# A two-layer hybrid decoder trunk on one core: gates computed with Tanh, one weight sum and two norm sums placed elsewhere

## The chip, the core and the metric

The kernel runs on one core of a Trainium2 chip. TensorE (PE) multiplies, VectorE (DVE) and ScalarE (ACT) work on elements, GpSimd (POOL) issues some transfers, and SyncE (SP) issues most of them through its own queue. The metric is the time of one execution on the device in microseconds; for the kernel before it is 2039.78 us, the median of three runs.

## The reference, cut to what matters

A sequence of 256 tokens of width 2048 goes through two layers. One input projection feeds three token mixers (A sparse attention, B a convolution module with a layer norm, C stick-breaking attention), a SiLU gate for each, and 3 x 2048 merge gates. All of it is float32.

```python
h = rms_norm(x, norm_w)
proj = h @ w_in                      # 2048 x 18064
(qa, ka, va, za, qi, ki, wi, ub, zb, qc, kc, vc, zc, gates) = split(proj)
y_a = (dsa_attention(...)            * silu(za)) @ w_a_out
y_b = (conformer_conv(ub, ...)       * silu(zb)) @ w_b_out
y_c = (stick_breaking_attention(...) * silu(zc)) @ w_c_out
g = sigmoid(gates).reshape(b, s, 3, 2048)
merged = g[:, :, 0] * y_a + g[:, :, 1] * y_b + g[:, :, 2] * y_c
x = x + merged @ w_out

# in conformer_conv, after the depthwise convolution (1024 channels):
y = layer_norm(y, ln_w, ln_b)        # mean, then mean of squares, over channels
```

## The kernel before

**Weight units.** Every product streams its weights. A unit is 256 x 512 weights, 128 partitions x 1024 floats, 512 KB. SP loads it into one of six `raw` buffers (`load_unit`, L270). ACT casts it into a high half (`high`, tile `wh`, L281), DVE subtracts that to get the low half (`low`, tile `wl`, L286), and PE makes three passes, high weight by both halves of the activations and low weight by their high half (`mult`, L297). There are three `wh` and three `wl` buffers, so a cast waits for PE to have read the `wh` three units back, and a load waits for DVE to have read the `raw` six units back. A regular unit has 12 matmuls of 512 columns.

**Work beside the stream.** Everything else (rotary, convolution, norms, attention) is written as generators. After each unit `background` lets one or two of them take a step; `yield n` says that the next step is due n units later. So the numbers behind `yield` place the work in the stream. The tile scheduler then sets the order of the instructions on each engine, by priority and by the ties that `issue_after` makes. A step that is placed on PE between two units stops the stream if its operands are not there yet.

**The norm of the convolution (`conv_norm`).** DVE folds eight channel groups into one tile, ACT writes its scaled high half (L1032, tile `ph`), DVE the low half, and `means` lets PE sum over partitions with a matrix of ones (L1038). That is done once for the mean and, after squaring (L1048), once for the mean of squares. Each time a `yield 3` stands between the fold and PE's sums. In the same stretch `attend` transposes the attention weights of mixer A by transfers (L994), and ACT copies the transposed halves back (L1002).

**Seven-product groups (`strassen`).** Three of the groups of merge-gate columns, `FAST = ((2, 0), (0, 0), (0, 1))`, each 1024 columns wide, are computed with seven products of blocks instead of eight. The activations are mixed once (`mix`); of the weights, sums of blocks are made on DVE (`summands`, L1195), then cast and split like a unit (`halves`). A product on such a block is 6 matmuls. The first half of a group runs four steps u, each with the blocks b11, b12 and b22 and with four products:

```python
product(o1, plain(0, 0), u, halves(b11));  s5 = summands(b11, b12);  yield 1
product(o5, mixed(0), u, halves(s5));      yield 2
b22 = block(KC, 512)                       # load
summands(s5, b22, dst=s6)                  # second sum, kept for the second half
product(o6, mixed(1), u, halves(s6));      s7 = summands(b12, b22);  yield 2
product(o7, mixed(3), u, halves(s7));      yield 2
```

After the four steps DVE and ACT combine the products (the first of the gates is activated at L1237); the second half has the other three products and activates the rest at L1254 and L1255. `combine` runs the regular units of the three branch outputs (`w_b`, `w_c`, `w_a`) and earns credit for each (`RATES`, 2.1 to 2.5 a unit); the group in turn spends it, `yield n` costing n. So a step with `yield 2` takes about the length of one regular unit.

**Gates.** The other merge-gate columns are regular units, and ACT applies the Sigmoid at L962 (`early_steps`). `combine` multiplies a branch's output by its gate and sums up (L1161, L1163, L1164). The SiLU gates of the branches are made in `gate_steps` (Silu at L439, product at L441). The stick-breaking heads (`stick`, two heads a call from h0) need Abs, Exp and Ln, and after each Abs the kernel asks for the table set with exp and ln (L770). ACT holds one set of function tables; where the next function is in another, an ACT_TABLE_LOAD stands in its order.

Of the kernel before, what the change touches and what calls it, by code (L numbers as in the profile page):

```python
# [53 lines left out]
def trunk(ctx: ExitStack, tc: tile.TileContext, x, xt, w_in, w_a, w_b, w_c, w_out,  # L54
          fnw, consts, out):
    nc = tc.nc
# [378 lines left out]
    def gate_steps(c0, o, b, w, hx, done, park=None, slots=(True, True), turn=TURN, need=(), ks=(0, 4)):  # L435
        def gated(k, z, v):
            for e in need:
                complete(e)
            nc.scalar.activation(v, z, AF.Silu)  # L439
            yield 1  # L440
            nc.vector.tensor_mul(z, v, o[:, k:k + 4, :])  # L441
            yield 1
            if park is None:
                b.extend(parts(4))
                h_, l_ = hi(b, k, 4), lo(b, k, 4)
            else:
                h_, l_ = v.bitcast(F32R), z.bitcast(F32R)
            nc.scalar.copy(h_, z)
            yield 1
            nc.vector.tensor_sub(l_, z, h_.bitcast(F32))  # L450
            if park is not None:
                for i, v_ in enumerate((h_, l_)):
                    nc.gpsimd.dma_start(park[:, k:k + 4, i], v_)

        for k in ks:
            a = yield from chunk_steps(w, [(c0 + k * P, 512)], hx, KD, whole=True)
            done.append(turn_in(a, None, partial(gated, k), slots[k // 4], turn))
# [66 lines left out]
    for layer in range(DEPTH):  # L524
# [234 lines left out]
        def stick(h0, qcT=qcT, kcT=kcT, vcr=vcr, diag=diag):  # L759
            ps = mm_tile()  # L760
            for q in range(2):
                nc.tensor.matmul(ps[:, q * S:(q + 1) * S], kcT[:, h0 + q, 0:P], qcT[:, h0 + q, :],
                                 start=True, stop=True)
            for q in range(2):
                nc.tensor.matmul(ps[:, 512 + q * P:512 + (q + 1) * P], kcT[:, h0 + q, P:S],
                                 qcT[:, h0 + q, P:S], start=True, stop=True)
            nk, lb = t4(), t4()
            ab = nc.scalar.activation(nk[:, :768], ps[:, :768], AF.Abs)
            with tc.issue_after(ab.ins):
                nc.scalar.preload_act_table_set("natural_log_exp_and_others")  # L770
            nc.scalar.activation(nk[:, :768], nk[:, :768], AF.Exp, scale=-1.0)
            yield 1
            nc.scalar.activation(nk[:, :768], nk[:, :768], AF.Ln, bias=1.0)
            yield 1
            nc.vector.scalar_tensor_tensor(lb[:, :768], ps[:, :768], 0.0, nk[:, :768],
                                           op0=ALU.min, op1=ALU.subtract)
            nc.vector.scalar_tensor_tensor(nk[:, :768], ps[:, :768], 0.0, nk[:, :768],
                                           op0=ALU.max, op1=ALU.add)
            yield 1
            for d in diag(nk):  # L780
                nc.vector.tensor_mul(d, d, smask2)
            pr_ = pair(768)
            nc.scalar.copy(pr_[0], nk[:, :768])
            yield 1
            nc.vector.tensor_sub(pr_[1], nk[:, :768], pr_[0].bitcast(F32))
            yield 3
            pc = mm_tile()
            for i, v in enumerate(pr_):
                nc.tensor.matmul(pc[:, :512], upper_r, v[:, :512], start=i == 0, stop=False)
            for i, v in enumerate(pr_):  # L790
                nc.tensor.matmul(pc[:, :512].rearrange("p (h t) -> p h t", h=2)[:, :, P:S], ones_r,
                                 v[:, 512:768].rearrange("p (h t) -> p h t", h=2), start=False, stop=i == 1)
            for i, v in enumerate(pr_):
                nc.tensor.matmul(pc[:, 512:768], upper_r, v[:, 512:768], start=i == 0, stop=i == 1)
            nc.vector.tensor_sub(lb[:, :768], lb[:, :768], pc[:, :768])
            yield 1
            nc.scalar.activation(lb[:, :768], lb[:, :768], AF.Exp)
            yield 1
            for d in diag(lb):
                nc.vector.tensor_mul(d, d, smask2)  # L800
            yield 2
            po = mm_tile()
            for q in range(2):
                vs_ = slice((h0 + q) * P, (h0 + q + 1) * P)
                nc.tensor.matmul(po[:, q * S:(q + 1) * S], vcr[:, 0, vs_], lb[:, q * S:(q + 1) * S],
                                 start=True, stop=False)
                nc.tensor.matmul(po[:, q * S + P:(q + 1) * S], vcr[:, 1, vs_],
                                 lb[:, 512 + q * P:512 + (q + 1) * P], start=False, stop=True)
            nc.scalar.copy(qcT[:, h0:h0 + 2, :], po[:, :512].rearrange("p (h t) -> p h t", h=2))
# [147 lines left out]
        def early_steps(b, j):  # L957
            a = yield from chunk_steps(w, [(O_G + b * D + j * 512, 512)], hx, KD)
            sg_ = t4().rearrange("p (t d) -> p t d", t=NT)
            with tc.high_priority():  # L960
                for t in range(NT):
                    nc.scalar.activation(sg_[:, t, :], a[t], AF.Sigmoid)  # L962
            nc.gpsimd.dma_start(gates[b][:, :, j * 512:(j + 1) * 512].rearrange("t p d -> p t d"), sg_)  # L963

        def attend(t, c, qaT=qaT, kaT=kaT, va=va, bias=bias):
# [56 lines left out]
        def conv_norm(cv=cv, pr=pr):  # L1022
            work = t4()
            ph_ = pair(512)[0]

            def fold(w_, first, second):
                w4 = w_.rearrange("p (c t) -> p c t", c=4)
                nc.vector.tensor_add(w4, first, second)
                nc.vector.tensor_add(w_[:, :512], w_[:, :512], w_[:, 512:])
                nc.vector.tensor_add(w_[:, :S], w_[:, :S], w_[:, S:2 * S])  # L1030
                h, l = ph_[:, :S], ph_[:, S:2 * S]
                nc.scalar.activation(h, w_[:, :S], AF.Copy, scale=1.0 / CW)  # L1032
                nc.vector.scalar_tensor_tensor(l, w_[:, :S], 1.0 / CW, h.bitcast(F32), op0=ALU.mult, op1=ALU.subtract)

            def means():
                ps = mm_tile()
                for i in range(2):
                    nc.tensor.matmul(ps[:, :S], ones_r, ph_[:, i * S:(i + 1) * S], start=i == 0, stop=i == 1)  # L1038
                return ps

            fold(work, cv[:, :4, :], cv[:, 4:, :])
            yield 3
            ps = means()
            sq = [t4().rearrange("p (c t) -> p c t", c=4) for _ in range(2)]
            for i in range(2):
                cs = cv[:, i * 4:i * 4 + 4, :]
                nc.vector.tensor_sub(cs, cs, heads(ps[:, :S], 4))
                nc.scalar.activation(sq[i], cs, AF.Square)  # L1048
                yield 1
            fold(work, *sq)  # L1050
            yield 3
            vs = means()
            r = rsqrt_mean(vs[:, :S], 1, t4())
            for i in range(2):
                cs = cv[:, i * 4:i * 4 + 4, :]
                yield 1
                nc.vector.tensor_mul(cs, cs, heads(r, 4))
                yield 1
                for c in range(4):
                    cc = i * 4 + c  # L1060
                    lw, lb = pr[:, P_LW + cc:P_LW + cc + 1], pr[:, P_LB + cc:P_LB + cc + 1]
                    nc.scalar.activation(cs[:, c, :], cs[:, c, :], AF.Silu, bias=lb, scale=lw)
# [70 lines left out]
        def combine():  # L1133
# [6 lines left out]
            for n, b in enumerate((1, 2, 0)):  # L1140
# [7 lines left out]
                for j in range(4):  # L1148
# [9 lines left out]
                    with tc.high_priority():  # L1158
                        dst = mg[j // 2][:, j % 2]
                        if n == 0:  # L1160
                            nc.vector.tensor_mul(dst, y, sg_)  # L1161
                        else:
                            nc.vector.tensor_mul(sg_, y, sg_)  # L1163
                            nc.vector.tensor_add(dst, dst, sg_)  # L1164
                    if n == 2 and j < 3:
                        mx[j], = parts(4)
# [37 lines left out]
        def strassen(b, jj):  # L1204
# [4 lines left out]
            for u in range(4):  # L1209
# [5 lines left out]
                s5 = summands(b11, b12)  # L1215
                yield 1
                product(o5, mixed(0), u, halves(s5))
                yield 2
                b22 = block(KC, 512)
                s6 = tp.tile([P, 1024], F32, tag=("ph", "pl")[u % 2], bufs=2, name=nm("s6")).rearrange(  # L1220
                    "p (k c) -> p k c", k=2)
                summands(s5, b22, dst=s6)
                kept.append(s6)
                product(o6, mixed(1), u, halves(s6))
                s7 = summands(b12, b22)
                yield 2
# [4 lines left out]
            with tc.high_priority():  # L1231
# [2 lines left out]
                nc.vector.tensor_sub(c12, o5, c21)  # L1234
                nc.vector.tensor_add(c21, o7, c21)  # L1235
                nc.vector.tensor_sub(c22, o5, c21)
                nc.scalar.activation(c22, c22, AF.Sigmoid)  # L1237
            yield 3
            pc, pd = mm_tile(), mm_tile()
            o2, o4, o3 = pc[:, :512], pc[:, 512:], pd[:, :512]  # L1240
# [9 lines left out]
            with tc.high_priority():  # L1250
                nc.vector.tensor_add(c11, o2, c11)
                nc.vector.tensor_add(c21, o4, c21)
                nc.vector.tensor_add(c12, o3, c12)
                nc.scalar.activation(res[0], res[0], AF.Sigmoid)  # L1254
                nc.scalar.activation(c12, c12, AF.Sigmoid)  # L1255
            if (b, jj) == fast[-1]:
                kept_res.extend(res)
                return
# [150 lines left out]
```

## Time and profile before

| | |
|---|---|
| median of three runs | 2039.78 us (2039.72 to 2040.48) |
| the profiled execution | 2038.03 us |
| its span, first to last instruction | 2036.3 us |
| mean granted TensorE clock | 0.997 |
| PE busy | 2009.3 us, 9518 matmuls |
| DVE busy | 1630.7 us |
| ACT busy | 1420.3 us, of it 31 table loads of 1.28 us |

In the listings a row names the line, the engine and the operation, then output<-inputs by the program's names, and the shape. A row of the timeline begins with the start and the length in us and may end with the idle time before it and what released it. A row of the windows has the window, its length, and for PE, PE's weight loads, DVE, ACT and POOL the busy time and the number of instructions, then the granted clock, the busy share of the DMA engines and the GB/s moved. A row of waits reads "engine, line waiting <- what ended the wait: us in total, times, longest". The first groups of the two layers run from about 605 and 1615 us, the norms' sums stand at about 526 and 1536 us.

### The profile page before, as it was taken

The page shows a single profiled execution, that of the slowest core. Times are in us where ns is not written, and L with a number is a line of the kernel's source. Part 1 is how long each engine was busy: PE and PEld are TensorE (multiplying, and loading weights), DVE is VectorE, ACT ScalarE, POOL GpSimd, SP SyncE. Part 2 cuts the span into 40 slices and gives each one's busy share as a digit, 9 for nine tenths or more (in the row PEclk, how much of TensorE's full clock was granted, in tenths as well). Part 3 has the DMA queues.
Part 4 walks back from the last instruction along what each step waited for, and adds up shares of the span by engine and source line. Part 5 has one row for each costly group of instructions (what it writes and reads, how often), then busy time and mean ns, then how long its engine had stood idle before and what let it go on. Part 6 is the DMA issues. An engine that isn't in the chain of part 4 may idle for free. (4 is left out here: it accounts for less than half of the span.)

```text
span 2036.3 us, 26826 instructions
## 1 busy us (share of the span) xinstructions
PE 2009.3 (99%) x9518; PEld 1684.6 (83%) x9518; DVE 1630.7 (80%) x1778; ACT 1420.3 (70%) x2000; POOL 102.9 (5%) x168
## 2 busy tenths in 40 slices
PE   9999999999999999999999999999999999999998
PEld 7888889988787788778888888899887877887787
DVE  8688767888898888896676887688887987889865
ACT  7699767559876656566657997675698756555653
POOL 0000000000000112200000000000000001212000
PEclk9999999999999999999999999999999999999999
DMA  8788657667898788889867775676777987889883
GB/s 282 214 226 217 178 157 227 206 198 200 213 262 243 247 272 290 281 251 262 257 202 219 212 214 168 170 224 197 206 203 211 271 254 238 269 289 296 245 273 126
DMA packets 349750, 466.98 MB, mean 229 GB/s; under 512 B 109360, under 2 KB 167472, under 8 KB 349488
## 3 DMA queue, kind: packets, MB, share of 16 engines
q1 hardware_dynamic: 329216, 425.01, 71.0%
q0 software_dynamic: 18944, 37.75, 6.2%
q10 hardware_dynamic: 1456, 2.51, 0.4%
q8 instruction: 74, 1.21, 0.3%
q14 instruction: 60, 0.49, 0.1%
HBM read 419.59 MB, written 23.07 MB: 217 GB/s over the span
## 5 line engine op out<-in xcount | busy, mean ns | idle before, releaser
L297 PE MATMUL acc<-wh,s 128*128 128x512 f32 (+2 forms) x4480 | 1099.2, 386 | 1.9 <-ACT wh L281 1.9
L286 DVE TENSOR_TENSOR wl<-raw,wh 128x1024 fp32r<-128x1024 f32 (+2 forms) x706 | 847.4, 1208 | 268.8 <-ACT wh L281 241.2
L297 PEld LDWEIGHTS acc<-wh,s 128*128 128x128 f32 x4480 | 828.1, 188 | 174.2 <-ACT wh L281 8.7
L281 ACT CAST wh<-raw 128x1024 fp32r<-128x1024 f32 (+2 forms) x705 | 729.6, 1039 | 320.7 <-PE acc L297 264.4
L297 PE MATMUL acc<-wl,s 128*128 128x512 f32 (+2 forms) x2240 | 590.7, 385 | 0.4 <-DVE wl L286 0.3
L297 PEld LDWEIGHTS acc<-wl,s 128*128 128x128 f32 x2240 | 415.0, 188 | 85.6 <-DVE wl L286 2.8
L476 ACT ACTIVATE t<-s,cst 128x255 f32<-128x255 f32 (+14 forms) x480 | 200.6, 488 | 0.0
L297 PE MATMUL mm<-wh,s 128*128 128x512 f32 x672 | 186.6, 397 | 10.2 <-ACT wh L281 8.7
L297 PEld LDWEIGHTS mm<-wh,s 128*128 128x128 f32 x672 | 124.7, 188 | 47.7 <-ACT wh L281 21.1
L479 DVE TENSOR_TENSOR s<-s,t 128x1020 f32<-128x1020 f32 (+14 forms) x120 | 138.6, 1155 | 1.9 <-ACT t L476 1.3
L297 PE MATMUL acc<-s,wh 128*128 128x384 f32 (+1 forms) x608 | 126.3, 348 | 0.0
L281 ACT CAST wh<-s 128x1024 fp32r<-128x1024 f32 x48 | 50.3, 1048 | 101.3 <-DVE s L1195 80.5
L297 PEld LDWEIGHTS acc<-s,wh 128*128 128x128 f32 x608 | 104.4, 189 | 3.2
L297 PE MATMUL mm<-wl,s 128*128 128x512 f32 x336 | 105.2, 394 | 0.3 <-DVE wl L286 0.3
L281 ACT CAST wh<-t 128x1024 fp32r<-128x1024 f32 x48 | 50.4, 1051 | 72.8 <-DVE t L1195 68.0
L286 DVE TENSOR_TENSOR wl<-s,wh 128x1024 fp32r<-128x1024 f32 x48 | 58.8, 1224 | 36.5 <-ACT wh L281 36.0
L297 PE MATMUL acc<-s,wl 128*128 128x192 f32 (+1 forms) x608 | 80.5, 273 | 0.0
L297 PEld LDWEIGHTS acc<-s,wl 128*128 128x128 f32 x608 | 79.5, 191 | 1.0
L297 PEld LDWEIGHTS mm<-wl,s 128*128 128x128 f32 x336 | 63.0, 189 | 15.0 <-DVE wl L286 1.5
L286 DVE TENSOR_TENSOR wl<-t,wh 128x1024 fp32r<-128x1024 f32 x48 | 58.8, 1224 | 20.0 <-ACT wh L281 19.0
L963 POOL DMA_DIRECT2D gates<-t x12 | 8.9, 742 | 1098.8 <-ACT t L962 1098.8
L248 POOL COPY sm<-sm 128x3 f32<-128x3 f32 x68 | 43.8, 652 | 400.7 <-ACT sm L247 400.7
(251 smaller groups left out, 1329.5 us busy)
## 6 DMA issues: line engine op xcount, KB each, us to landing
raw<-in_w_in_dram SPq DMA_DIRECT2D x578, 512.0 KB, 4.4
raw<-in_w_out_dram SPq DMA_DIRECT2D x64, 512.0 KB, 5.4
raw<-in_w_b_dram SPq DMA_DIRECT2D x32, 512.0 KB, 5.4
raw<-in_w_c_dram SPq DMA_DIRECT2D x32, 512.0 KB, 5.1
raw<-in_w_a_dram SPq DMA_DIRECT2D x32, 512.0 KB, 5.7
t<-gates POOLq DMA_DIRECT2D x20, 512.0 KB, 6.7
s<-parked POOLq DMA_DIRECT2D x32, 256.0 KB, 6.3
gates<-t POOLq DMA_DIRECT2D x12, 512.0 KB, 6.4
```

Of the source, the lines that this page charges most:

```text
L248: seen = nc.gpsimd.tensor_copy(copy[:, :3], mark)
L281: highs[0] = nc.scalar.copy(u[1], u[0])
L286: sub = nc.vector.tensor_sub(u[2], u[0], u[1].bitcast(F32))
L297: newest[0] = nc.tensor.matmul(o, lhsT, rhs, start=start, stop=stop, skip_group_check=True)
L476: nc.scalar.activation(o[:, i, :S - d], yT[:, c, :S - d], AF.Copy, scale=wq)
L479: sums.append(lambda: nc.vector.tensor_add(to, to, o[:, :, :S - d]))
L963: nc.gpsimd.dma_start(gates[b][:, :, j * 512:(j + 1) * 512].rearrange("t p d -> p t d"), sg_)
```

## The change

Four edits, with the same result up to rounding.

1. The merge gates are computed as tanh(x/2) in place of the sigmoid, which is (1 + tanh(x/2)) / 2. The 1 is added where the gate multiplies the branch's output, by a fused operation with the same number of instructions, and the factor 1/2 goes into the SiLU gate's product (L441), also a fused operation.
2. The request for the exp-and-ln tables in the stick-breaking heads stands only at h0 = 0.
3. In the first half of a seven-product group the load of b22 and the second sum stand ahead of the `yield 2` that was between the second and the third product.
4. The two `yield 3` ahead of the norm's sums become `yield 5`.

```diff
 gate_steps:
-            nc.vector.tensor_mul(z, v, o[:, k:k + 4, :])
+            nc.vector.scalar_tensor_tensor(z, v, 0.5, o[:, k:k + 4, :], op0=ALU.mult, op1=ALU.mult)
 stick:
-            with tc.issue_after(ab.ins):
-                nc.scalar.preload_act_table_set("natural_log_exp_and_others")
+            if h0 == 0:
+                with tc.issue_after(ab.ins):
+                    nc.scalar.preload_act_table_set("natural_log_exp_and_others")
 early_steps:
-                    nc.scalar.activation(sg_[:, t, :], a[t], AF.Sigmoid)
+                    nc.scalar.activation(sg_[:, t, :], a[t], AF.Tanh, scale=0.5)
 conv_norm, twice:
-            yield 3
+            yield 5
 combine:
-                            nc.vector.tensor_mul(dst, y, sg_)
+                            nc.vector.scalar_tensor_tensor(dst, sg_, 1.0, y, op0=ALU.add, op1=ALU.mult)
...
-                            nc.vector.tensor_mul(sg_, y, sg_)
+                            nc.vector.scalar_tensor_tensor(sg_, sg_, 1.0, y, op0=ALU.add, op1=ALU.mult)
 strassen:
                 product(o5, mixed(0), u, halves(s5))
-                yield 2
                 b22 = block(KC, 512)
...
                 summands(s5, b22, dst=s6)
                 kept.append(s6)
+                yield 2
                 product(o6, mixed(1), u, halves(s6))
...
-                nc.scalar.activation(c22, c22, AF.Sigmoid)
+                nc.scalar.activation(c22, c22, AF.Tanh, scale=0.5)
...
-                nc.scalar.activation(res[0], res[0], AF.Sigmoid)
-                nc.scalar.activation(c12, c12, AF.Sigmoid)
+                nc.scalar.activation(res[0], res[0], AF.Tanh, scale=0.5)
+                nc.scalar.activation(c12, c12, AF.Tanh, scale=0.5)
```

The number of matmuls is the same, and so is that of DVE's, POOL's and SP's instructions; on ACT 18 of the 31 table loads are gone (L770 has 2 in place of 8, L962 2 in place of 6, L980, L1062 and L1237 none in place of 4, 2 and 2), and on DVE 36 plain multiplies have become fused ones. From L771 on the changed kernel's lines are numbered one higher.

The first place is ACT at the end of the first half of the first group in layer 1. L1237 and L962 (now L1238 and L963) are gates, L439 is the Silu of a branch's gate, `wh_...<-s_976` (now `s_973`) is the cast of a second sum. Before:

```order
L281 CAST wh_6007<-raw_6005 128x1024
L1237 ACT_TABLE_LOAD
L1237 ACTIVATE t_1039_5937<-t_1039_5937 128x512
L281 CAST wh_6018<-raw_6017 128x1024
L188 COPY t_1003_5774<-t_1004_5775 128x1024
L281 CAST wh_6040<-raw_6038 128x1024
L439 ACT_TABLE_LOAD
L439 ACTIVATE t_1004_5775<-t_1003_5774 128x1024
L962 ACT_TABLE_LOAD
L962 ACTIVATE t_1064_6061<-acc_5778 128x512
L281 CAST wh_6051<-s_976_5647 128x1024
```

and with the change:

```order
L281 CAST wh_6015<-raw_6014 128x1024
L188 COPY t_1003_5771<-t_1004_5772 128x1024
L1238 ACTIVATE t_1039_5934<-t_1039_5934 128x512
L281 CAST wh_6037<-raw_6035 128x1024
L439 ACTIVATE t_1004_5772<-t_1003_5771 128x1024
L281 CAST wh_6048<-s_973_5625 128x1024
L281 CAST wh_6074<-raw_6073 128x1024
L247 COPY sm_6067<-wh_6048 128x3
L963 ACTIVATE t_1064_6058<-acc_5775 128x512
```

The three loads are gone, and the gate of L963 stands behind the cast of the sum and one more.

The second place is DVE in the second step of the first group. `wl_...` are lows, `t_969` is the first sum (s5), `s_976` (now `s_973`) the second (s6), `t_979` the third (s7); the low from `raw_5626` (now `raw_5627`) belongs to a regular unit. Before:

```order
L286 TENSOR_TENSOR wl_5605<-raw_5600,wh_5604 128x1024
L1195 TENSOR_TENSOR t_969_5614<-raw_5600,raw_5602 128x1024
L286 TENSOR_TENSOR wl_5617<-t_969_5614,wh_5616 128x1024
L286 TENSOR_TENSOR wl_5628<-raw_5626,wh_5627 128x1024
L1195 TENSOR_TENSOR s_976_5647<-t_969_5614,raw_5645 128x1024
L286 TENSOR_TENSOR wl_5650<-s_976_5647,wh_5649 128x1024
L1195 TENSOR_TENSOR t_979_5659<-raw_5602,raw_5645 128x1024
```

and with the change:

```order
L286 TENSOR_TENSOR wl_5602<-raw_5597,wh_5601 128x1024
L1196 TENSOR_TENSOR t_969_5611<-raw_5597,raw_5599 128x1024
L286 TENSOR_TENSOR wl_5614<-t_969_5611,wh_5613 128x1024
L1196 TENSOR_TENSOR s_973_5625<-t_969_5611,raw_5623 128x1024
L286 TENSOR_TENSOR wl_5629<-raw_5627,wh_5628 128x1024
L286 TENSOR_TENSOR wl_5647<-s_973_5625,wh_5646 128x1024
L1196 TENSOR_TENSOR t_979_5656<-raw_5599,raw_5623 128x1024
```

The second sum stands ahead of the regular unit's low; on SP the load of its block (`raw_5645`, now `raw_5623`) stands ahead of the regular unit's load in the same way.

The third place is ACT and PE at the norm of layer 1. On ACT before (`ph_4711`, now `ph_4708`, is the scaled copy; `wh_4816`, `wh_4840` and `wh_4881` are casts of the fifth, sixth and eighth unit of a block of the regular stream, now `wh_4806`, `wh_4835` for the fifth and sixth):

```order
L281 CAST wh_4840<-raw_4839 128x1024
L991 COPY t_800_4720<-t_782_4625 128x512 x3
L281 CAST wh_4863<-raw_4862 128x1024
L991 COPY t_800_4720<-t_782_4625 128x512
L1002 COPY t_770_4563<-t_771_4564 128x512 x2
L281 CAST wh_4881<-raw_4880 128x1024
L1032 ACTIVATE ph_4711<-t_797_4710 128x256
```

and with the change:

```order
L1003 COPY t_770_4560<-t_771_4561 128x512
L281 CAST wh_4806<-raw_4805 128x1024
L992 COPY t_800_4717<-t_782_4622 128x512 x4
L281 CAST wh_4835<-raw_4834 128x1024
L1003 COPY t_770_4560<-t_771_4561 128x512
L1033 ACTIVATE ph_4708<-t_797_4707 128x256
```

The scaled copy stands behind the cast of the sixth unit instead of the eighth; one of the copies of transposed words is directly ahead of it. PE's sums stood after three and after eight matmuls of the sixth unit (`wh_4840`):

```order
L297 MATMUL acc_4725<-wl_4817,s_10_101 128x512 x4
L297 MATMUL acc_4725<-wh_4840,s_10_101 128x512 x3
L1038 MATMUL mm_4784<-ph_4711,ones_r 128x256
L297 MATMUL acc_4725<-wh_4840,s_10_101 128x512 x5
L1038 MATMUL mm_4784<-ph_4711,ones_r 128x256
```

and stand now ahead of it:

```order
L297 MATMUL acc_4722<-wl_4807,s_10_101 128x512 x4
L1039 MATMUL mm_4827<-ph_4708,ones_r 128x256 x2
L297 MATMUL acc_4722<-wh_4835,s_10_101 128x512 x8
```

So, counted in units of this block, the sums stand on PE three to eight matmuls earlier than before, with the larger number behind `yield`.

More of the change, by code (lines that the diff above doesn't have):

```diff
@@ L1050, in conv_norm @@
             fold(work, *sq)
-            yield 3
+            yield 5
             vs = means()
```

## The prediction

> **What bounds the kernel.** I read the mean granted clock and the busy shares first, then the busy time by windows of 100 us, then the waits of the engine that bounds, and at last the timeline around its longest waits.
>
> ```profile
> core 0: 2036.3 us, clock 0.997
> PE 2009.3 (99%) x9518; PEld 1684.6 (83%) x9518; DVE 1630.7 (80%) x1778; ACT 1420.3 (70%) x2000; POOL 102.9 (5%) x168
> ```
>
> TensorE (PE) is busy in 99% of the span, and PE's matmuls are counted with modelled ends, so a busy share near 100% still hides lost time. The number of matmuls in a window is the sharper measure (columns: PE busy and count, weight loads, VectorE (DVE), ScalarE (ACT), POOL, granted clock, DMA share, GB/s):
>
> ```profile
> 100.00:200.00 100.00, 100.00 (x443) 82.81 (x442) 82.47 (x75) 96.60 (x178) 0.00 (x0) 1.00 0.83 221
> 600.00:700.00 100.00, 95.71 (x400) 74.30 (x399) 84.72 (x78) 65.46 (x69) 4.32 (x7) 0.98 0.81 240
> 700.00:800.00 100.00, 99.76 (x438) 81.57 (x437) 85.46 (x77) 56.02 (x71) 20.47 (x33) 1.00 0.83 267
> 800.00:900.00 100.00, 98.52 (x427) 79.20 (x426) 89.83 (x81) 56.42 (x73) 19.84 (x34) 1.00 0.92 293
> 1600.00:1700.00 100.00, 95.42 (x399) 74.13 (x398) 85.35 (x82) 65.98 (x70) 5.50 (x8) 0.98 0.83 235
> 1700.00:1800.00 100.00, 99.76 (x438) 81.62 (x437) 87.78 (x79) 55.57 (x69) 18.64 (x30) 1.00 0.86 280
> 1800.00:1900.00 100.00, 98.73 (x429) 79.31 (x428) 89.25 (x81) 57.32 (x76) 21.96 (x37) 1.00 0.90 288
> ```
>
> The undisturbed pace is 443 matmuls per 100 us, 0.226 us each. The windows with the first seven-product group (600 to 700 and 1600 to 1700) lack 43 and 44 matmuls, 87 x 0.226 = 19.7 us. The four windows with the second and third groups lack 5, 16, 5 and 14, that is 40 x 0.226 = 9.1 us (both counts from above, since a few records may be missing). That is all there is to win in the groups. What PE waits for by name (us in total, times, longest):
>
> ```profile
> PE mm L297 <- ACT wh L281: 8.7, 13, 2.3
> PE mm L1038 <- ACT ph L1032: 4.4, 2, 2.8
> PE acc L297 <- ACT wh L281: 1.9, 7, 0.3
> SPq L270 <- DVE wl L286: 1117.7, 553, 7.4
> ACT wh L281 <- DMA raw<-in_w_in_dram: 8.9, 6, 1.7
> ```
>
> PE waits for ScalarE's casts and twice for the norm's folded sum. The transfer queue waits 1117.7 us for free buffers, and the casts wait for transfers only 8.9 us: transfers run ahead.
>
> **Part one: gates by Tanh, 18 table loads fewer.** ACT has slack on the whole (70%), so a load counts only where PE waits for the cast behind it. There is one such place in each layer, at the end of the first half of the first group:
>
> ```profile
> 676.65 1.28 ACT L439 ACT_TABLE_LOAD   x1
> 677.94 1.06 ACT L439 ACTIVATE t<-t 128x1024 f32<-128x1024 f32 x1
> 678.04 1.07 PE L297 MATMUL mm<-wh,s 128*128 128x512 f32 x4
> 679.02 1.28 ACT L962 ACT_TABLE_LOAD   x1
> 680.32 0.60 ACT L962 ACTIVATE t<-acc 128x512 f32<-128x512 f32 x1
> 680.81 1.04 ACT L281 CAST wh<-s 128x1024 fp32r<-128x1024 f32 x1
> 681.90 1.53 PE L297 MATMUL mm<-wh,s 128*128 128x512 f32 x4 [2.34 <-ACT wh L281]
> 1692.54 1.78 PE L297 MATMUL mm<-wh,s 128*128 128x512 f32 x4 [2.34 <-ACT wh L281]
> 680.00:690.00 10.00, 8.10 (x28) 6.47 (x29) 6.82 (x7) 7.25 (x10) 1.83 (x3) 0.83 0.62 160
> 1530.00:1540.00 10.00, 7.25 (x33) 5.65 (x32) 7.92 (x11) 7.42 (x11) 0.00 (x0) 1.00 0.88 221
> 1690.00:1700.00 10.00, 7.66 (x27) 6.02 (x27) 6.90 (x7) 7.89 (x10) 1.77 (x3) 0.83 0.58 143
> ```
>
> Two loads (2 x 1.28 = 2.56 us) and the gate's first ACTIVATE (0.60) stand between the Silu and the cast that PE waits for, 2.34 us in each layer. In the changed order both loads are gone and the gate's ACTIVATE stands behind that cast. So the cast starts 3.1 us earlier; 2.34 us are needed. Right behind, the granted clock is 0.83 over 10 us, which is half clock for 3.4 us, a loss of 1.7 us. Without the idle the clock has no reason to drop: 2.34 + 1.7 = 4.1 us a layer, **8.2 us**. Bounds: 4.7 (idle alone) to 8.2.
>
> Here the Trainium skill, page "ScalarE: Activation LUTs", section "What ACT_TABLE_LOAD costs", speaks of about 1380 ns of drain beside the 1283 ns of the load. The rows above show no drain (677.94 follows 676.65 + 1.28 at once), so the measurement decides. By the page's 2.66 us a switch, an estimate, 18 loads would give ACT 47.9 us, against 18 x 1.28 = 23.1 by the rows.
>
> The other 14 loads I cost at nothing: the loads of the stick-breaking heads and of the early gates stand where PE lacks no matmul (443 per 100 us), under PE's 2.72 us a unit. If that cover failed, a load would be worth 1.28 us: at most 14 x 1.28 = 17.9 us, which I don't believe, since PE's list of waits has no such sum. A Tanh of 128x512 is priced like the Sigmoid it replaces, and the fused multiply like the plain one:
>
> ```profile
> L962 ACT ACTIVATE t<-acc 128x512 f32<-128x512 f32 x24 | 13.9, 594 | 4.3 <-PE acc L297 4.2
> L974 DVE SCALAR_TENSOR_TENSOR t<-mm,bias 128x1024 f32<-128x1024 f32 x4 | 4.9, 1222 | 4.1 <-DMA gates<-t 4.1
> L1163 DVE TENSOR_TENSOR t<-acc,t 128x1024 f32<-128x1024 f32 x16 | 19.5, 1220 | 0.5 <-PE acc L297 0.5
> ```
>
> 36 of them by 2 ns are 0.07 us: nothing.
>
> **Part two: the second sum a step sooner.** In each of the four steps of a group's first half DVE makes the second sum just before ACT casts it:
>
> ```profile
> 624.15 1.22 DVE L1195 TENSOR_TENSOR s<-t,raw 128x1024 f32<-128x1024 f32 x1
> 625.48 1.05 ACT L281 CAST wh<-s 128x1024 fp32r<-128x1024 f32 x1 [1.74 <-PE acc L297]
> 626.58 1.20 PE L297 MATMUL mm<-wh,s 128*128 128x512 f32 x4 [0.23 <-ACT wh L281]
> 637.56 1.20 PE L297 MATMUL mm<-wh,s 128*128 128x512 f32 x4 [0.79 <-ACT wh L281]
> ```
>
> Sum, cast and product are a chain with no room: the cast ends at 626.53, and PE starts 0.05 us later, after 0.23 us of idle. Now the sum stands ahead of the regular unit's low between (1.22 us), so the chain begins that much sooner. Nothing is added, DVE does the same 7 operations per step; the change moves work. What it pays: the 19.7 us of the first groups less the 8.2 above leave 11.5; part of it belongs to the first and third sums, which do not move (637.56 waits for a first sum). I take about two thirds, **7.5 us**, since the freed ACT time and the earlier sum both shorten these chains; bounds 0 and 11.5. Of the 9.1 us of the later groups I take **1.5** (bounds 0 and 5), because there PE's waits by name are tenths.
>
> Its cost: b22's raw load (SP's queue) moves ahead of a regular unit's load in 24 steps (4 steps, 3 groups, 2 layers). I put **1.5 us** as new stalls here (bounds 0 and 27, priced under the rivals); what covers it is the lead of the transfers above.
>
> **Part three: the norm's sums two units later.** PE's two matmuls for the mean stand in the middle of a unit, and their operand comes late:
>
> ```profile
> 519.17 2.32 SPq L994 DMA_TRANSPOSE t<-t  x1
> 524.79 0.76 ACT L1002 COPY t<-t 128x512 uint16<-128x512 uint16 x1 [1.31 <-DMA t<-t]
> 525.42 1.03 ACT L281 CAST wh<-raw 128x1024 fp32r<-128x1024 f32 x1
> 526.36 0.41 ACT L1032 ACTIVATE ph<-t 128x256 fp32r<-128x256 f32 x1
> 526.83 0.39 PE L1038 MATMUL mm<-ph,ones_r 128*128 128x256 f32 x1 [1.61 <-ACT ph L1032]
> 1537.20 0.39 PE L1038 MATMUL mm<-ph,ones_r 128*128 128x256 f32 x1 [2.75 <-ACT ph L1032]
> ```
>
> ACT's scaled copy stood behind a copy that waits for a transpose (1.31 us) and behind the cast of a unit two places ahead. Now it follows the cast of the sixth unit, with one such copy between, whose transposes SP issues earlier, and the sums stand behind the fifth unit on PE. I take the whole wait, **4.4 us**; bounds 4.4 and -1.4 (the first of the two, now 3 matmuls nearer the front, waits 3 x 0.226 = 0.7 us longer in each layer).
>
> **Sum.** 8.2 + 7.5 + 1.5 + 4.4 - 1.5 = 20.1 us. The profiled execution took 2038.03 us, 1.7 us of it outside the span, and lies 1.75 us under the median 2039.78. So the profile after should read 2017.9, and the median **2019.7**; with the first groups' sums between 3.5 and 11 us in place of 7.5 the likeliest case runs from 2016 to 2024.
>
> **Rivals.**
>
> Only the loads and the norm pay (15%). DVE is the cover here, 85 to 90% busy in all group windows, and a reordered sum only pushes the next low back by 1.22 us: what the second product gains the regular unit's low loses. Then 8.2 + 4.4 = 12.6 us stay, 2027.2. For it: DVE's count is unchanged, 84.72 of 100 us in the worst window. Against: every named wait of a product there is for ACT's cast, not for DVE's low.
>
> The norm's wait stays (15%): a transposed copy like the one that ACT waited 1.31 us for still stands directly ahead of the scaled copy. Then PE, which comes to its sums earlier, pays 1.4 more instead of 4.4 less, and the sum is 20.1 - 4.4 - 1.4 = 14.3, 2025.5. Against: the scaled copy stands two casts earlier, and the transposes leave SP earlier.
>
> The clock drops all the same (4%): the 3.4 us at half clock follow a 2.34 us idle, yet no drop followed 2.75 us at 1534 to 1537, where the granted clock is 1.00. So idle length alone does not decide, and shorter stalls could still bring it: 20.1 - 3.4 = 16.7, 2023.1. The Trainium skill, page "TensorE: Matmul & The Clock Gate", Part 1, has a free-running window of about 3.4 us, after whose idleness the rate halves; the trace has the 3.4 us, but a 2.34 us idle sufficed.
>
> Slower, through the transfer queue (9%). A unit's load lands 4.4 us after issue, and 512 KB at the mean rate take 524,288 B / 229 GB/s = 2.3 us:
>
> ```profile
> DMA packets 349750, 466.98 MB, mean 229 GB/s; under 512 B 109360, under 2 KB 167472, under 8 KB 349488
> raw<-in_w_in_dram SPq DMA_DIRECT2D x578, 512.0 KB, 4.4
> ```
>
> In 24 steps b22's load now goes ahead of a regular unit's, with six raw buffers for both, so that unit's weights come up to 2.3 us later. If half of it, 1.15 us, comes out uncovered, 24 x 1.15 = 27.5 us are lost: 2019.7 + 27.5 = 2047.2. It turns the whole change slower from 20.1 / 24 = 0.84 us a step. For it: DMA is 81 to 92% busy in these windows. Against: the casts' 8.9 us of waits for transfers in the whole span.
>
> **Chances.** Likeliest case 57%, the three milder rivals 15, 15 and 4%, the slower one 9%. A measurement of this kernel tells 0.2% (4.1 us, so below 2035.7 or above 2043.9) from no change. Faster by more: 57 + 15 + 15 + 4 = 91%. Of the slower rival two thirds lie above 2043.9: 6%, and 3% within. The range that should hold the time 8 times in 10 reaches down to the sums' full 11.5 us with 2 us more in the later groups (20.1 + 6 = 26.1, 2013.7) and up to the first rival with the half clock kept as well (2027.2 + 3.4 = 2030.6): 2013.5 to 2031.
>
> **What would show it.** Right: no wait of over 1 us of a product for ACT's cast near 676 to 684, granted clock 1.00 in that window, no wait of L1038's successor for the scaled copy, 13 table loads on ACT, and some 435 matmuls in the windows of the first groups (4.1 + 3.75 us are 35 more than 400). The sums' term is wrong if the count there rises by only 18, the 4.1 us of the loads and the clock, while the second products no longer wait; the slower rival shows as casts that wait for raw transfers, by tens of us. The forecast falls if the first groups lack as many matmuls as now, or if the stall at the norm only moves to the next unit.

## The result, and the profile after

The changed kernel takes 2011.84 us (median, 2011.18 to 2013.56), the kernel before 2039.75 us in the same comparison: a ratio of 0.9866, with an interval of 0.9849 to 0.9883, so 27.9 us faster. Faster was forecast, by 20.1 us; the time lies 1.7 us below the range. The profiled execution after took 2011.18 us, 26.85 us less than the one before.

First the granted clock, the busy shares, and the windows of 100 us around the norms (500, 1500) and the groups (columns as before: window, length, PE busy and count, weight loads, DVE, ACT, POOL, clock, DMA share, GB/s):

```profile
core 0: 2009.4 us, clock 0.999
PE 1997.0 (99%) x9518; PEld 1685.5 (84%) x9518; DVE 1626.4 (81%) x1778; ACT 1399.2 (70%) x1982; POOL 110.0 (5%) x168
500.00:600.00 100.00, 100.00 (x444) 82.75 (x443) 87.23 (x96) 82.89 (x113) 3.79 (x6) 1.00 0.87 236
600.00:700.00 100.00, 99.63 (x434) 80.57 (x433) 90.69 (x84) 67.70 (x75) 8.41 (x15) 1.00 0.87 262
700.00:800.00 100.00, 100.00 (x443) 82.76 (x442) 87.22 (x79) 57.90 (x74) 21.97 (x35) 1.00 0.87 279
800.00:900.00 100.00, 99.23 (x432) 80.16 (x431) 91.78 (x84) 58.78 (x70) 17.43 (x24) 1.00 0.87 276
1600.00:1700.00 100.00, 99.58 (x434) 80.55 (x433) 90.99 (x84) 66.81 (x75) 9.17 (x15) 1.00 0.87 263
1700.00:1800.00 100.00, 100.00 (x442) 82.78 (x442) 88.54 (x80) 58.44 (x74) 21.11 (x33) 1.00 0.88 282
1800.00:1900.00 100.00, 99.63 (x434) 80.73 (x433) 92.35 (x84) 59.98 (x71) 17.43 (x24) 1.00 0.88 274
```

The windows of the first groups went from 400 and 399 matmuls to 434 each, as expected (435). The windows from 700 and 1700 are at the undisturbed pace, which was not expected to that extent. ACT is less busy by 21.1 us, close to the 23.1 of the loads. What PE's products still wait for by name:

```profile
PE mm L297 <- ACT wh L281: 0.9, 3, 0.5
PE acc L297 <- ACT wh L281: 0.9, 3, 0.5
```

The timeline at the end of the first half of the first group, and at the norm of layer 1:

```profile
668.84 1.05 ACT L439 ACTIVATE t<-t 128x1024 f32<-128x1024 f32 x1
670.11 1.22 DVE L1196 TENSOR_TENSOR s<-s,raw 128x1024 f32<-128x1024 f32 x1
671.34 1.07 PE L297 MATMUL acc<-wl,s 128*128 128x512 f32 x4
671.41 1.05 ACT L281 CAST wh<-s 128x1024 fp32r<-128x1024 f32 x1 [1.52 <-DVE s L1196]
672.24 1.07 PE L297 MATMUL mm<-wh,s 128*128 128x512 f32 x4
673.41 0.59 ACT L963 ACTIVATE t<-acc 128x512 f32<-128x512 f32 x1
...
520.14 0.81 ACT L1003 COPY t<-t 128x512 uint16<-128x512 uint16 x1
520.77 0.45 ACT L1033 ACTIVATE ph<-t 128x256 fp32r<-128x256 f32 x1
524.02 0.40 PE L1039 MATMUL mm<-ph,ones_r 128*128 128x256 f32 x2
```

The cast at 671.41 no longer stands behind loads and the gate. It waits 1.52 us for DVE's sum, and PE goes on without a gap. At the norm the scaled copy is done at 521.2 and PE reads it at 524.0, 2.8 us later. The list of waits has no row for L1039.

For the comparison of many kernels I use one figure by stage: the time by which matmuls start later after the one before than at the undisturbed pace of their form, summed over the stage and both layers. It is worked out from the start times in each profile, so from one execution of each kernel, which lies up to 2.5 us off the kernel's median. "Rest" is nearly the same everywhere and belongs to other stages. Counted instead by when the matmul of the same number starts in the profiles before and after, the norms gain 1.9 and 3.1 us in the two layers, the first groups 7.8 and 8.0, the later groups 2.7 and 2.9: a stage's figure is good to about 0.8 us.

| lost time in us | norm | first groups, first half | its end | second groups, first half | up to the third groups' end | rest | sum |
|---|---|---|---|---|---|---|---|
| before | 7.8 | 9.8 | 10.1 | 2.2 | 7.9 | 26.9 | 64.7 |
| the change | 2.0 | 4.1 | 0.0 | 0.0 | 5.1 | 27.0 | 38.1 |
| gates only (e1) | 5.5 | 9.9 | 2.2 | 2.8 | 7.7 | 26.7 | 54.8 |
| second sum only (e2) | 6.8 | 4.1 | 1.7 | 0.1 | 5.8 | 27.2 | 45.6 |
| yields only (e3) | 9.4 | 9.5 | 10.4 | 2.2 | 7.7 | 27.1 | 66.3 |
| gates and sum (e4) | 4.4 | 4.1 | 0.0 | 0.1 | 5.1 | 27.1 | 40.7 |
| gates and yields (e5) | 2.8 | 9.9 | 1.8 | 2.9 | 7.8 | 26.6 | 51.7 |
| sum and yields (e6) | 6.6 | 4.1 | 1.7 | 0.0 | 5.2 | 27.3 | 44.9 |
| b22's load only (e7) | 10.0 | 8.9 | 11.2 | 4.3 | 8.0 | 27.0 | 69.4 |
| the change and first sum (e8) | 1.8 | 0.1 | 0.0 | 0.0 | 3.1 | 27.2 | 32.1 |
| first sum only (e10) | 8.3 | 5.1 | 9.4 | 0.0 | 3.1 | 26.6 | 52.4 |
| e8 and fourth sum (e11) | 2.0 | 1.1 | 0.0 | 1.0 | 3.9 | 27.0 | 34.9 |

### The profile page after: what moved, and what is told of

Its sections match the earlier page's. It is cut to its first block, busy times and chain, and to the rows that moved or that the text cites. A ratio compares the mean times of both kernels' runs of the same rounds, so it can differ in the third digit from the quotient of the medians.

```text
span 2009.4 us, 26811 instructions
## 1 busy us (share of the span) xinstructions
PE 1997.0 (99%) x9518; PEld 1685.5 (84%) x9518; DVE 1626.4 (81%) x1778; ACT 1399.2 (70%) x1982; POOL 110.0 (5%) x168
## 4 chain that ended last, share of the span: by engine, by line
PE 93%; DVE 3%; ACT 1%; issue 1%; DMA 1%; ACTq 0%; DVEq 0%; SPq 0%
PE acc L297 80%; PE mm L297 10%; DVE wl L286 1%; ACT wh L281 1%; DMA raw<-in_w_c_dram 1%; DVE t L1196 1%; PE mm L941 1%; PE mm L971 1%; PE mm L1011 0%; DVE s L1196 0%; PE mm L806 0%; PE mm L762 0%; DMA raw<-in_w_in_dram 0%; PE mm L915 0%; PE mm L790 0%
## 5 line engine op out<-in xcount | busy, mean ns | idle before, releaser
L297 PE MATMUL mm<-wh,s 128*128 128x512 f32 x672 | 182.2, 391 | 1.1 <-ACT wh L281 0.9
L248 POOL COPY sm<-sm 128x3 f32<-128x3 f32 x68 | 51.4, 765 | 382.0 <-ACT sm L247 382.0
```

The costliest lines, as they stand in the source:

```text
L248: seen = nc.gpsimd.tensor_copy(copy[:, :3], mark)
L297: newest[0] = nc.tensor.matmul(o, lhsT, rhs, start=start, stop=stop, skip_group_check=True)
```

## The experiments

The change has three parts that can be taken apart: the gates with their table loads (edits 1 and 2), the second sum with its block's load (edit 3), the yields (edit 4). The theory of the prediction is that each pays at its own place. The rival is that they stand in for one another or need one another. Six kernels make all combinations, with before and the change. Each is compared with the kernel before on its own chip; differences below are to that median.

**Gates only.** Edits 1 and 2 on the kernel before.

```diff
-  nc.scalar.activation(sg_[:, t, :], a[t], AF.Sigmoid)
+  nc.scalar.activation(sg_[:, t, :], a[t], AF.Tanh, scale=0.5)
...
+  if h0 == 0:
```

> The kernel before with the gates by Tanh and the 18 table loads gone, the second sum and the yields of the norm as before. If the parts pay each at its own place (the prediction): the 2.34 us idle and the half clock at the end of the first groups go (8.5 us with the small gaps around), the second sums stay late, the norm's wait stays: about 8.5 us under before, 2031. If the freed ScalarE time is what the second sums lacked, the first groups' other gaps close as well: 15 to 18 us under before, 2022 to 2025. In its order the norm's scaled copy stands behind the sixth cast but PE's sums stand inside the fourth unit, so the norm's wait should not be smaller than 4.4 us.

Measured: 2027.94 against 2037.7, 9.8 us under (ratio 0.9953, 0.9938 to 0.9968). The end of the first groups' first half loses 2.2 in place of 10.1, the first halves keep their 9.9. Windows, a wait and the timeline of this kernel:

```profile
600.00:700.00 100.00, 98.00 (x418) 76.50 (x417) 87.48 (x80) 63.31 (x68) 6.18 (x8) 1.00 0.86 252
PE mm L1039 <- ACT ph L1033: 2.1, 2, 1.2
676.14 1.22 DVE L1196 TENSOR_TENSOR s<-s,raw 128x1024 f32<-128x1024 f32 x1
677.44 1.05 ACT L281 CAST wh<-s 128x1024 fp32r<-128x1024 f32 x1 [1.18 <-DVE s L1196]
677.50 1.07 PE L297 MATMUL mm<-wh,s 128*128 128x512 f32 x4
678.87 1.07 PE L297 MATMUL mm<-wh,s 128*128 128x512 f32 x4
```

418 matmuls are 18 more than 400, which is 4.1 us, the number of the prediction for this place. The cast now waits for DVE's sum, not for ACT's loads, and it ends at 678.5, just ahead of the product. Freed ScalarE time alone gave the second sums nothing. The norm's wait fell to 2.1 us, although no fewer than 4.4 were expected: the scaled copy came forward by more than PE's sums did. In the traces the first of these sums stands 20 matmuls earlier than before, which is 4.5 us at the undisturbed pace, and the scaled copy is done at 521.77 in place of 526.77.

**Second sum only.** Edit 3 on the kernel before.

```diff
-                yield 2
                 b22 = block(KC, 512)
...
                 summands(s5, b22, dst=s6)
                 kept.append(s6)
+                yield 2
```

> The kernel before with b22's load and the second sum ahead of the yield, all 31 table loads and the norm as before. Parts at their own places: 6 us of the first groups and 5 us of the later groups, the idle at the end of the first half stays: about 11 us under before, 2029. If the sum's place also frees that idle (in its order the cast of the sum stands ahead of the gate's load and ACTIVATE, 1.28 + 0.60 us less before it, 2.34 needed), the 1.7 us of half clock goes with it: 11 + 2 x 3.6 = 18 us under before, 2022. The transfer-queue rival: slower than before by over 10 us.

Measured: 2021.17 against 2037.7, 16.5 us under (ratio 0.992, 0.9905 to 0.9935). The end of the first half again:

```profile
600.00:700.00 100.00, 99.35 (x431) 79.40 (x430) 90.04 (x83) 69.53 (x74) 6.12 (x10) 1.00 0.87 259
672.81 1.28 ACT L439 ACT_TABLE_LOAD   x1
673.96 1.22 DVE L1195 TENSOR_TENSOR s<-s,raw 128x1024 f32<-128x1024 f32 x1
674.10 1.06 ACT L439 ACTIVATE t<-t 128x1024 f32<-128x1024 f32 x1
675.27 1.05 ACT L281 CAST wh<-s 128x1024 fp32r<-128x1024 f32 x1
676.37 1.20 PE L297 MATMUL mm<-wh,s 128*128 128x512 f32 x4 [0.21 <-ACT wh L281]
677.29 1.28 ACT L962 ACT_TABLE_LOAD   x1
```

The table loads are all there, but the sum is done when its cast's turn comes, the cast stands ahead of the gate's load on ACT, and the 2.34 us idle is 0.21. No half clock follows. So the stall that the prediction laid on two table loads is cured by either part. The first halves lose 4.1 in place of 9.8, and the later groups 5.9 in place of 10.1 (both columns).

**Yields only.** Edit 4 on the kernel before.

```diff
-            yield 3
+            yield 5
```

> The kernel before with yield 5 for yield 3 in the norm, nothing else. Parts at their own places: the norm's waits go, 5 us under before, 2035. If the norm's wait is set by ScalarE's order and not by the yield: in this kernel's order the scaled copy still stands behind the eighth cast and PE's sums inside the sixth unit, as before, so 0 us, 2039.8 with the two waits of 1.6 and 2.8 us in the profile.

Measured: 2039.06 against 2037.7, no difference (ratio 1.0006, 0.9996 to 1.0015).

```profile
500.00:600.00 100.00, 97.53 (x425) 80.32 (x424) 85.68 (x93) 83.12 (x116) 3.75 (x5) 0.98 0.83 224
PE mm L1038 <- ACT ph L1032: 4.6, 2, 2.5
525.23 0.76 ACT L1002 COPY t<-t 128x512 uint16<-128x512 uint16 x1 [2.11 <-DMA t<-t]
525.86 1.03 ACT L281 CAST wh<-raw 128x1024 fp32r<-128x1024 f32 x1
526.80 0.41 ACT L1032 ACTIVATE ph<-t 128x256 fp32r<-128x256 f32 x1
527.26 0.39 PE L1038 MATMUL mm<-ph,ones_r 128*128 128x256 f32 x1 [2.47 <-ACT ph L1032]
```

The scaled copy still stands behind the copy that waits for its transpose and behind the eighth cast, and PE's sums inside the sixth unit. The later yield does not delay the first of them on PE, and the wait stays. The granted clock of 0.98 is a stretch at half clock behind the 2.47 us idle, which the kernel before does not have at this norm.

**Two parts at a time.** Gates and sum (edits 1 to 3), gates and yields (1, 2, 4), sum and yields (3, 4).

> The changed kernel without its yields (yield 3 in the norm). Everything but the norm: 27.9 less 5 = 23 us under before, 2017, with waits of PE's norm sums of 4 us or more. If the freed ScalarE alone repairs the norm: the changed kernel's time, 2012.

> The changed kernel without the move of the second sum (b22 and its sum behind the yield, as before). If the yields repair the norm only where the gates' loads are gone: the waits of PE's norm sums vanish here too (5.8 us under before) beside the 8.5 us of the first groups' ends, 14 us under before; the first half of the first groups keeps its 9.9 us of lost time and the later groups their 10. If the repair of the norm needs the sum as well: 10 us under before, like the gates alone, with waits of about 2 us or more at the norm.

> The changed kernel with the 31 table loads and the Sigmoid. If the yields do nothing while the loads are there: the same as the sum alone, 16.5 us under before, with 4 us of waits at the norm. If loads and sum pay each at its own place: 5 to 6 us less than that, 22 us under before, no wait at the norm.

Measured: gates and sum 2014.37 against 2037.7, 23.3 under (0.9888, 0.9872 to 0.9905); gates and yields 2025.08 against 2038.67, 13.6 under (0.9933, 0.9918 to 0.9948); sum and yields 2019.37 against 2038.67, 19.3 under (0.9906, 0.9889 to 0.9922). By the table, gates and sum leave 4.4 at the norm, gates and yields 2.8, sum and yields 6.6. With gates and sum the named waits at the norm are 1.9 us, less than the 4 expected, as with the gates alone. Windows with the norm, of gates and yields, then of sum and yields:

```profile
500.00:600.00 100.00, 100.00 (x444) 82.76 (x443) 87.42 (x96) 83.59 (x114) 3.75 (x5) 1.00 0.86 236
```

```profile
500.00:600.00 100.00, 97.73 (x433) 80.53 (x432) 87.12 (x95) 84.31 (x117) 3.75 (x5) 1.00 0.85 230
PE mm L1038 <- ACT ph L1032: 4.1, 2, 2.3
```

So the yields pay only where the loads are gone: 5.5 to 2.8 with the gates, 4.4 to 2.0 with gates and sum, some 2.5 us by the table (3.8 and 3.7 by the medians, across chips). With the gates the yields put the first of PE's sums 17 matmuls later, behind the scaled copy. The sum plays no part there. Sum and yields came 3 us better than the sum alone in the medians, but their intervals overlap and their profiles differ by 0.7 us in lost time and by 0.2 at the norm, so that I make nothing of it.

**b22's load only.** The load ahead of the yield, the sum behind it, on the kernel before.

```diff
-                yield 2
                 b22 = block(KC, 512)
+                yield 2
                 s6 = ...
```

> The kernel before with b22's load alone ahead of the yield; the second sum stays behind it, and DVE's and ScalarE's orders are as before. If the place of the sum on DVE pays: no gain here, within 2 us of before, the first halves keep 9.8 us of lost time. If the early load pays (the sum waited for its block): most of the 16 us of the sum alone show here. The transfer-queue rival: slower by 10 us or more, with casts that wait for raw transfers.

Measured: 2042.31 against 2038.67, slower by 3.6 us (1.002, 1.0011 to 1.003).

```profile
600.00:700.00 100.00, 95.66 (x400) 74.33 (x399) 85.41 (x79) 65.45 (x68) 4.07 (x6) 0.98 0.83 243
700.00:800.00 100.00, 99.42 (x433) 80.36 (x432) 85.05 (x77) 56.22 (x73) 20.71 (x33) 1.00 0.82 266
ACT wh L281 <- DMA raw<-in_w_in_dram: 4.7, 4, 1.7
```

The first group stays at 400 matmuls. So the gain of edit 3 is the place of the sum on DVE, not that of the transfer. The load alone costs 2.1 us in the second groups and, at the norm, 2.2, of which one more stretch at half clock is 1.7. Casts wait for raw transfers less than before (4.7 us for 8.9), so the slower rival's mechanism is not what costs it; what does is not settled.

**The first sum too.** What the change still loses in the first halves (4.1 us) are products of the first sum. It can be made ahead of b11's low half. This on the changed kernel, then on the kernel before alone, and the first with the fourth sum in the second half moved likewise; the changed kernel stood beside the latter two.

```diff
+                s5 = summands(b11, b12)
                 product(o1, plain(0, 0), u, halves(b11))
-                s5 = summands(b11, b12)
                 yield 1
```

```diff
+                s4 = summands(kept[u], b21, dst=kept[u])
                 product(o2, plain(0, KC), u, halves(b21))
-                s4 = summands(kept[u], b21, dst=kept[u])
                 yield 1
```

> The changed kernel with the first sum also sooner, ahead of the low half of b11. The first groups still lose 2 us each in their first halves, at products of the first sum. If the same rule holds (a sum that is late on DVE is what PE waits for): 1 to 3 us under the changed kernel's gain, 29 to 31 us under before. If b11's low half, now pushed back by 1.22 us, is the next to be late: the changed kernel's gain of 26 to 28 us or less, with products that wait for DVE's low half.

> The changed kernel itself, beside the two below on one chip, so that their distance to it is read from one place: 26 to 29 us under before.

> The kernel before with only the first sum sooner, ahead of b11's low half; the second sum, the loads and the norm as before. If each sum pays for its own product: of the 9.8 us that the first halves lose, the 4 us of the first sums go, 4 us under before. If the first sum's lateness also made the second late (it is its operand): the second sums' part goes too, 8 to 10 us in the first halves and some of the later groups' 10 us, 10 to 18 us under before; the idle at the end of the half stays unless that sum is early enough.

> The changed kernel with the first sum sooner as in the run before, and in the groups' second half the fourth sum ahead of b21's low half in the same way. What is left in the later groups is 3 us by the profile. If the fourth sum is what is late there: 1 to 2 us under the first sum's version (33.6 us under before). If b21's low half becomes the late one: 1 to 3 us above it.

Measured: the changed kernel again 2011.9 against 2038.87, 27.0 under (0.987, 0.9854 to 0.9887). With the first sum sooner 2005.02 against 2038.67, 33.7 under (0.9833, 0.9818 to 0.9847): it beats both kernels, and by more than the 29 to 31 expected, since beside the 4.0 us of the first halves 2.0 came back in the later groups. The first sum alone 2028.34 against 2038.87, 10.5 under (0.9951, 0.9936 to 0.9965). With the fourth sum as well 2008.75, 30.1 under (0.9855, 0.984 to 0.987), some 3 us worse than without, across chips. By the table 2.0 of that stand in the first halves of groups, where nothing was moved against the version without, and 0.8 up to the third groups' end; why is not shown. The changed kernel with the first sum:

```profile
600.00:700.00 100.00, 100.00 (x443) 82.75 (x442) 93.08 (x86) 69.64 (x76) 9.44 (x15) 1.00 0.89 268
PE acc L297 <- DVE wl L286: 1.0, 2, 0.8
```

The window of the first group is at the undisturbed pace, with DVE at 93%. Regular units wait twice for their low half (0.8 us at 851 us and 0.2); no product is named, so b11's low half, pushed back by the sum, is not the next to be late. The first sum alone, on the kernel before:

```profile
600.00:700.00 100.00, 97.06 (x411) 76.81 (x410) 87.10 (x80) 66.66 (x69) 5.77 (x8) 0.98 0.84 249
677.43 1.28 ACT L962 ACT_TABLE_LOAD   x1
679.22 1.04 ACT L281 CAST wh<-s 128x1024 fp32r<-128x1024 f32 x1
680.31 2.08 PE L297 MATMUL mm<-wh,s 128*128 128x512 f32 x4 [2.35 <-ACT wh L281]
```

DVE has made the second sum by 677.44, but its cast stands behind the gate's load and ACTIVATE in ACT's order, and the stall and the half clock are as before. With edit 3 alone the cast stands ahead of that load. The two runs together point to the cast's place on ACT, which follows from the sum's, as what cures the stall. In the first halves the two sums pay apart: 9.8 - 5.1 = 4.7 for the first, 9.8 - 4.1 = 5.7 for the second, both together 9.7. In the second groups' first half either is enough (2.2 to 0.1 or 0.0). In all the later groups the first sum alone leaves 3.1 of 10.1, less than the second sum's 5.9: more than half of its gain in the table (7.0 of 12.3) lies there. So neither expectation holds whole: the first halves came out as in the first of them, the total as in the second.

## Why the prediction was right and where it was wrong

| term | predicted | measured by stage |
|---|---|---|
| end of the first halves of the first groups | 8.2 | 10.1 |
| first halves of the first groups, the sums | 7.5 | 5.7 |
| later groups | 1.5 | 5.0 |
| norm | 4.4 | 5.8 |
| new stalls | -1.5 | 0 |
| elsewhere | 0 | 0.2 |
| profile to profile | 20.1 | 26.9 |

**The step that failed** is the one on the later groups: "Of the 9.1 us of the later groups I take 1.5 (bounds 0 and 5), because there PE's waits by name are tenths." The 9.1 us had been counted from matmuls that were lacking. The same count was trusted for the first groups and overruled here by the list of waits. 5.0 us came back, 3.5 more than put down, which is the upper bound that the text named. By the runs it came from the sum (2.2 to 0.1 and 7.9 to 5.8 with the sum alone, nothing with the gates alone).

The list shows only the time in which the profile has PE idle. In the later groups of the kernel before, the named waits are 2.1 and 1.4 us in the two layers, while 10.1 are lost by the table. The rest lies mostly around such waits and is counted as busy, because the ends of matmuls are modelled. One such place in the kernel before:

```profile
847.37 1.07 PE L297 MATMUL acc<-wl,s 128*128 128x512 f32 x4
848.84 1.21 PE L297 MATMUL mm<-wh,s 128*128 128x512 f32 x4 [0.40 <-ACT wh L281]
849.89 0.63 PE L297 MATMUL acc<-wh,s 128*128 128x512 f32 x2
```

Four matmuls take 0.90 us from start to start at the undisturbed pace (4 x 0.226). The product starts 1.47 us after the start of the four ahead of it, and what follows it starts 1.05 us later: some 0.7 us are lost where the list names 0.40.

**The range** was missed by this step together with the allowance for new stalls. Its low end took the sums' full 11.5 us but only 3.5 of the later groups, and kept the 1.5 us of new stalls. With 5.0 and none it would have reached 2010.7. The signs named for being right all showed (434 matmuls for some 435, 13 table loads, clock 1.00, no such wait), but they covered the first groups and the norm, not the later groups.

**New stalls** were put at 1.5 us, with the transfer queue as their source. None is seen; the named wait of casts for these transfers fell even where only the load was moved. That this move alone is 3.6 us slower shows that such an allowance was not absurd; whether the change pays some of it under the sum's gain is not shown.

**The norm** was sized by its named wait, 4.4, while the stage lost 5.8 more than after (5.0 counted by the matmul's number). The mechanism as told (the yields put the scaled copy behind an earlier cast) was half right. The order of the whole change was read, and what is due to the gates in it was laid on the yields: the gates alone bring the scaled copy forward, the yields alone do nothing, and only both remove the wait. Which of the 18 loads hold the copy back was not taken apart. The rival that the wait stays is refuted.

**The end of the first halves** was right in time and wrong in cause. 8.5 us at the stall and its half clock, 8.2 foretold; the other 1.6 are short gaps in the 10 us ahead of it, which the prediction had counted with the sums. The two first-group terms together are 15.7 foretold and 15.8 measured. But the stall was not the loads' alone: the earlier sum cures it with all loads in place. The working also misread its rows. Only one of the two loads stands between the Silu's ACTIVATE and the cast, and the cast could not start 3.1 us sooner on the old order of DVE, where the sum ends at 679.03, 1.8 us ahead of the cast:

```profile
677.81 1.22 DVE L1195 TENSOR_TENSOR s<-s,raw 128x1024 f32<-128x1024 f32 x1
```

With the gates alone the sum starts 1.4 us ahead of the product before it (676.14 and 677.50), in place of 0.2 (677.81 and 678.04), and so the cast comes in time. The first rival, "only the loads and the norm pay", is refuted the harder for it, since the sum alone gives 16.5 us and the gates alone 9.8. DVE's 85 to 90% was no cover that fails: it rose to 91% with the change and 93% with the first sum moved as well, and PE gained each time.

**The clock.** The rival that it drops all the same did not come true (1.00 in all windows of the groups). But its place in the sum, a fixed 1.7 us behind a long idle, was too simple. In these runs idles of 2.34 (before), 2.35 (first sum only), 2.47 (yields only) and 2.7 us (b22's load only) were followed by 3.4 us at half clock; idles at the norm of 2.75 (before), 2.5 (first sum only) and 2.3 us (second sum only) were not. The traces tell why. In each of these executions all changes of the granted clock stand on one raster of 3.413 us, while the program works: the two half-clock stretches before, for instance, start at 682.57 and 1692.92, 296 such steps apart. Windows on this raster in the kernel before, two at the stall, then two at the norm of layer 2:

```profile
679.16:682.57 3.41, 1.07 (x5) 0.58 (x4) 1.79 (x2) 3.40 (x4) 0.00 (x0) 1.00 0.54 158
682.57:685.98 3.41, 3.41 (x10) 2.60 (x9) 3.41 (x4) 2.69 (x5) 1.83 (x3) 0.50 0.20 30
1532.49:1535.90 3.41, 1.96 (x9) 1.30 (x7) 2.29 (x4) 1.69 (x4) 0.00 (x0) 1.00 1.16 269
1535.90:1539.32 3.42, 2.12 (x10) 1.74 (x11) 2.46 (x3) 2.74 (x5) 0.00 (x0) 1.00 0.48 151
```

The 2.34 us fall into one window, and the next one is at half clock. The 2.75 us are cut by an edge into 1.45 and 1.30, and the clock stays. In the four kernels with such stretches all ten of them followed a window in which PE idled 2.07 us or more. No window with 1.79 us or less was followed by one in any kernel, and nothing lies between. The Trainium skill, page "TensorE: Matmul & The Clock Gate", Part 1, has the window of about 3.4 us run freely, so that its phase would decide; these traces agree. Whether an idle of this length costs the 1.7 us is thus in part chance, and no run here sets the phase.

**The rest of the miss** is the step from profile to median. The profile before lay 1.75 us under its median, that after 0.7 us under, so 1.1 us of the 7.9 between 2019.7 and 2011.84 are noise of one profiled execution. The other 6.8 are the terms above.

## What to carry to other kernels

Size a stall by what the bound engine's instruction count lacks against its own undisturbed stretch, and use the list of waits to find the cause, not the size. Where a cast or a sum stands just ahead of its use on a nearly full engine, moving it one place forward can pay although the engine does no less work, and either end of such a chain may cure the same stall, so the parts' gains don't add up. When several edits change the order together, read the order of each edit alone before a gain is laid on one of them.

## What was not expected of the hardware

A DVE that is 93% busy in a window of 100 us held PE at its undisturbed 443 matmuls, so there the order of its work mattered and not how much of it there was. And the half clock followed a 2.34 us idle but not one of 2.75 us: what decided was how much of the idle fell into one window of the 3.413 us raster, with the limit between 1.79 and 2.07 us.
